# A hybrid encoder layer: raw weights in quarters, gate work moved into branch B, branch A and the output from the last block to the first

## The chip, the cores and the metric

One core of a Trainium2 chip runs the whole layer in one launch. The metric is the device time of one execution in microseconds, median of several runs. The engines are named as in the profile: PE (TensorE matmul), PEld (TensorE weight load), DVE (VectorE), ACT (ScalarE), POOL (GpSimd), SP (SyncE, which here issues every DMA on one queue).

## The reference, cut to what matters

Sequence 2048, model width 1024, float32 throughout, one layer.

```
h    = layer_norm(x)
proj = h @ w_in            # 1024 x 7592, cut into a_*, i_*, b_*, c_* and gate columns
# A: scores of an indexer (8 heads of 32), the 256 best keys of each query,
#    softmax over these; 8 heads of 64 that share one key and one value head
# B: 4 heads, each with two softmaxes p0, p1 over all allowed keys:
#    a = p0 - lam * p1;  o_b = rms_norm(a @ v)          (values 128 wide)
# C: 4 heads of 128, softmax over 256 memory tokens
# allowed keys: s < (t // 64 + 1) * 64, so block b of 128 queries sees (b + 1) * 128 keys
y_r  = (o_r * silu(gate_r)) @ w_proj_r                  for r in A, B, C
merged = sum over r of sigmoid(m_gate_r) * y_r
out  = layer_norm(2 ** 0.25 * h + merged @ w_out)
```

## The kernel before

The 2048 tokens are 16 blocks of 128 queries, or 8 pairs. Every product of the projections is done as three matmuls on a high and a low part (`mm3`, L74 to L77): the weights are read from DRAM in float32 into a raw tile `wr`, and split into `w` by two instructions (`split`, L64 to L72; L67 or L69 makes the high part, L72 the low one). `load_win` (L225) does that for a group of 256 columns: two halves of 512 rows, each one DMA of 512 KB into a raw tile of which there is one buffer, and a split by POOL (in the first part of the kernel ACT makes the high part). The split tile `w` has two buffers, so a group can be loaded while the one before it is in use.

A group of gate columns is a generator, `gate_steps` (L257): 2 x 2 x 8 = 32 steps of three matmuls 128x512, each counted as 0.69 us. There are 20 such groups for each half of the tokens (`JOBS`). Their results go to DRAM (`sg_d`, `tm_d`, `cq_d`).

Order of the program: layer norm and projections of the first half, the indexer's top-k by bisection (`topk_group`), the projections of the second half, top-k of the other blocks, the 20 gate groups of the second half, the first 4 of the first half, then branch B, branch A with what is left of the gates, the memory projections, branches C and B's output (`gated_b`, `gated_c`, called B/C below), and the final stage.

Within branch B (L795 on) the order of TensorE is written out by hand (`manual_schedule`): units of a head and a block, from block 15 to 0, for head 0 to 3. Between their steps `pump` puts gate steps: a unit of block b asks for 3.2 + 0.08 (b + 1) us of them (`FILL`), the first unit's eight logit steps for 0.5 us each. Ten gate groups are kept for this (`GB = (4, 10)`); when they are used up, `pump` does nothing.

Everywhere else a planner sets the order on each engine, SP's queue included: it simulates the program and takes, of the instructions that are ready in the simulation, the one that stands earliest in the program. So the remaining gates, the memory part and B/C, which stand behind branch A in the program, are taken where branch A leaves an engine free. The order so found is fixed: on the chip each engine works it off in turn.

Branch A (`attn_a`, L836) does a block of queries for 8 heads: logits, exponentials, transposes and products with the values. Its pools lie on the right side of the memory, those of B/C and of the first part of the final stage on the left. The final stage has two parts: `stage1(p)` (L1027) needs branch A's output of the pair p (`oa_d`) and the sum of B/C (`mg_d`), and `stage2(b)` (L1082) multiplies by `w_out` and normalizes. The first four `stage1` (`EARLY`) are written so that they need only the left side, whose pools of B/C must have been released; everything after them needs branch A's space as well.

Of the kernel before, what the change touches and what calls it, by code (L numbers as in the profile page):

```python
# [9 lines left out]
F32 = mybir.dt.float32  # L10
# [25 lines left out]
GV = 3  # L36
AHEAD = 1
EARLY = 4
WO = (1, 1)
YT = 8  # L40
YO = 1
APR = 2
GB = (4, 10)
FILL = (3.2, 0.08)
SQ_SCALE = 2.0 ** -80
SQ_LIM = 3.4028234663852886e38 * SQ_SCALE
# [10 lines left out]
def tile_layer(ctx, tc, x, mem, ln_in_g, ln_in_b, w_in, w_mem_kv, diff_lambda, diff_norm_g,  # L57
# [167 lines left out]
    def load_win(cols, eh=G, el=G, rpool=None):  # L225
        w = dw.tile([128, 2, KT, 256], F32R, name="w")
        n = sum(c for _, c in cols)
        for i in range(2):
            if rpool is None:
                raw = dw.tile([128, 4, 256], F32, name="wr", bufs=1)  # L230
            else:
                raw = rpool.tile([128, 4, 256], F32, name="wr")
            o0 = 0
            for c0, cn in cols:
                SP.dma_start(raw[:, :, o0:o0 + cn], w_view(w_in, i * 512, 4, c0, cn))
                o0 += cn
            split(w[:, 0, 4 * i:4 * i + 4, :n], w[:, 1, 4 * i:4 * i + 4, :n], raw[:, :, :n], eh, el)
        return w

    def dense(kind, half, cols, idx, w=None):  # L240
# [25 lines left out]
    def dense_ai01(half):  # L266
        W = []
        for i in range(2):
            if half == 0 and i:
                w = xw.tile([128, 2, 4, W_AI], F32R, name="w1", bufs=1)  # L270
            else:
                w = dw.tile([128, 2, KT, 256], F32R, name="w")
                w = w.rearrange("p a k c -> p (a k c)")[:, :8 * W_AI].rearrange("p (a k c) -> p a k c", a=2, k=4)
            W.append(w)
            for c0, cols in ((0, [(C_AK, 128), (C_IQ, 128)]), (256, [(C_IQ + 128, W_AI - 256)])):
                n = sum(c for _, c in cols)
                raw = dw.tile([128, 4, 256], F32, name="wr", bufs=1)
                o0 = 0
                for a0, an in cols:
                    SP.dma_start(raw[:, :, o0:o0 + an], w_view(w_in, i * 512, 4, a0, an))  # L280
                    o0 += an
                split(w[:, 0, :, c0:c0 + n], w[:, 1, :, c0:c0 + n], raw[:, :, :n], A if half == 0 else G, G)
        for p in range(4 * half, 4 * half + 4):
            ps = [dqs.tile([128, 512], F32, name="dps") for _ in range(2)]
            for a in range(2):
                for i in range(2):
                    h = hT_of(2 * p + i)
                    for k in range(4):
                        kk = 4 * a + k
                        mm3(ps[i][:, :W_AI], h[:, 0, kk], h[:, 1, kk], W[a][:, 0, k], W[a][:, 1, k], kk == 0, kk == KT - 1)  # L290
            with tc.high_priority():
                o = [dw.tile([128, 2, 256], F32, name="do", bufs=3) for _ in range(2)]
                with tc.high_priority():
                    for i in range(2):
                        A.copy(o[0][:, i], ps[i][:, :256])
                        A.copy(o[1][:, i, :W_AI - 256], ps[i][:, 256:W_AI])
                emit("ai0", None, p, None, 256, o[0])
                emit("ai1", None, p, None, W_AI - 256, o[1])
# [82 lines left out]
    def gates(half, jobs, between=()):  # L381
        between = list(between)
        for i, (kind, c0, idx) in enumerate(jobs):
            yield from gate_steps(kind, half, c0, idx)
            if between:
                between.pop(0)()

    def run(steps):
        for _ in steps:
# [12 lines left out]
    def dense_mem(j):  # L402
        w = dw.tile([128, 2, KT, 256], F32R, name="w")
        for i in range(2):
            raw = dw.tile([128, 4, 256], F32, name="wr", bufs=1)
            SP.dma_start(raw, w_view(w_mem_kv, i * 512, 4, 256 * j, 256))
            split(w[:, 0, 4 * i:4 * i + 4], w[:, 1, 4 * i:4 * i + 4], raw, G, G)
        ps = dqs.tile([128, 2, 256], F32, name="dps")
        for i in range(2):
            c = slice(i * 128, (i + 1) * 128)  # L410
            if j < 2:
                for k in range(KT):
                    mm3(ps[:, i], w[:, 0, k, c], w[:, 1, k, c], hm[0][:, 0, k], hm[0][:, 1, k], k == 0, k == KT - 1)
            else:
                for k in range(KT):
                    mm3(ps[:, i], hm[0][:, 0, k, c], hm[0][:, 1, k, c], w[:, 0, k], w[:, 1, k], k == 0, k == KT - 1)
        for i in range(2):
            o = dw.tile([128, 2, 256], F32R, name="do", bufs=3)
            if j < 2:
                split(o[:, 0], o[:, 1], ps[:, i], A, V)  # L420
                SP.dma_start(mk_d[:, 2 * j + i], o.bitcast(F32))
            else:
                h0 = 2 * (j - 2)
                ov = o.rearrange("p a (h d) -> p (a h d)", d=128).rearrange("p (h a d) -> p h a d", h=2, a=2)
                pv = ps[:, i].rearrange("p (h d) -> p h d", d=128)
                split(ov[:, :, 0], ov[:, :, 1], pv, A, V)
                SP.dma_start(mv_d[:, i, h0:h0 + 2].rearrange("p h a d -> p (h a d)"),
                             o.bitcast(F32).rearrange("p a c -> p (a c)"))
# [366 lines left out]
        load_v(0, g)  # L795
    units = [unit_b(hd, b) for hd in range(4) for b in range(NB - 1, -1, -1)]
    with tc.manual_schedule(engines={PE.engine}):
        for _ in units[0].logits():
            pump(0.5)
        units[0].mix()  # L800
        ahead = 1
        for i, u in enumerate(units):
            new = []
            while ahead < len(units) and ahead <= i + 2 and sum(x.slots for x in units[i:ahead + 1]) <= PB:
                new.append(units[ahead])
                ahead += 1
            share = FILL[0] + FILL[1] * (u.b + 1)
            m = 2 * (u.b // 4 + 1)
            n = sum(2 * (x.b // 4 + 1) for x in new)
            lg = (None for x in new for _ in x.logits())  # L810
            j = 0
            nxt = units[i + 1] if i + 1 < len(units) else None
            for t, _ in enumerate(u.values()):
                pump(share / m)
                while (j + 1) * m <= (t + 1) * n:
                    next(lg)
                    j += 1
                if t == m // 2 and nxt is not None and nxt not in new:
                    nxt.mix()
            for _ in lg:  # L820
                pass
            u.store()
            if nxt in new:
                nxt.mix()
# [67 lines left out]
            V.tensor_tensor(oo, oo, rc[:, 4 * h4:4 * h4 + 4, None].to_broadcast([128, 4, 64]), op=ALU.mult)  # L892
        SP.dma_start(oa_d[b], o.rearrange("p h d -> p (h d)"))

    for b in [7, 0, 6, 1, 5, 2, 4, 3, 8, 9, 10, 11, 12, 13, 14, 15]:
        attn_a(b)

    run(fill)
# [143 lines left out]
        return [ap.tile([128, 2, 256], F32, name="facc", bufs=bufs) for _ in range(4)]  # L1042

    wo = []
    for p in range(EARLY):
        acc = accs(fs, 3)
        stage1(p, acc)
        for u in range(4):
            SP.dma_start(mg_d[p][:, 2 * u:2 * u + 2], acc[u])
        if p == WO[0]:  # L1050
            wo += load_w(HW[:, 1], fs, "facc", w_out, 0, 3)
        if p == WO[1]:
            wo += load_w(fw.tile([128, 4, 2, D], F32R, name="wo2"), fs, "facc", w_out, 4, 3)

    aps.release()
# [8 lines left out]

    MT = {}

    def ready(p):
        if p >= NP:
            return
        acc = accs(fp, 4)  # L1070
        if p < EARLY:
            for u in range(4):
                SP.dma_start(acc[u], mg_d[p][:, 2 * u:2 * u + 2])
        else:
            stage1(p, acc)
        MT[p] = fp.tile([128, 2, KT, 256], F32R, name="fmT", bufs=AHEAD + 1)
        for u in range(4):
            H, L = (MT[p][:, a, 2 * u:2 * u + 2] for a in range(2))
            A.activation(H, acc[u], AF.Copy, scale=0.5)
            V.scalar_tensor_tensor(L, acc[u], 0.5, H.bitcast(F32), op0=ALU.mult, op1=ALU.subtract)  # L1080

    def stage2(b):  # L1082
        hh = fp.tile([128, D], F32, name="fh", bufs=3)
        SP.dma_start(hh, h_d[b])
        mT = MT[b // 2][:, :, :, 128 * (b % 2):128 * (b % 2) + 128]
        nz = 4 if b == NB - 1 else 2
        for n in range(nz):
            c = slice(n * (D // nz), (n + 1) * (D // nz))
            z = fq.tile([128, 512], F32, name="fz")[:, :D // nz]
# [1 line left out]
                mm3(z, mT[:, 0, k], mT[:, 1, k], wo[k][:, 0, c], wo[k][:, 1, c], k == 0, k == KT - 1)  # L1091
            V.scalar_tensor_tensor(hh[:, c], hh[:, c], ALPHA, z, op0=ALU.mult, op1=ALU.add)
        mu, rs = norm_stats(fp, hh, nz)
        if b < NB - 1:
            V.tensor_scalar(hh, hh, mu, rs, op0=ALU.subtract, op1=ALU.mult)
            G.tensor_tensor(hh, hh, gln, op=ALU.mult)
            V.tensor_tensor(hh, hh, bln, op=ALU.add)
            SP.dma_start(out[b * 128:(b + 1) * 128, :], hh)
            return
# [6 lines left out]
        ready(p)  # L1106
    for p in range(NP):
        ready(p + AHEAD)
        stage2(2 * p)
        stage2(2 * p + 1)  # L1110
    fq.release()
    fp.release()
    fqr.release()
# [52 lines left out]
```

## Time and profile before

| | us |
|---|---|
| median of 3 runs (lowest, highest) | 3029.1 (3028.67, 3036.97) |
| the profiled execution's own time | 3025.77 |
| its span in the profile | 3024.0 |
| PE busy | 2800.9 (93%) |
| DVE busy | 2165.2 (72%) |
| ACT busy | 1400.3 (46%) |
| POOL busy | 1068.0 (35%) |
| mean granted clock of TensorE | 0.97 of full |

A busy time is the sum over an engine's instructions as the profiler recorded them; matmuls are pipelined and their ends are modelled. The granted clock is told as a share of 2.4 GHz; the two levels seen are full (2.4 GHz) and half (1.2 GHz).

### The profile page before, as it was taken

The numbers are of one execution on the slowest core, as the hardware profiler recorded it, in microseconds if no ns is written. First come the engines' busy times: TensorE is split into PE (matmuls) and PEld (weight loads), VectorE is DVE, ScalarE is ACT, GpSimd is POOL, SyncE is SP. The second block draws the span as 40 slices with busy tenths as digits, with TensorE's granted clock in tenths as the row PEclk, the third lists the DMA queues.
The fourth block names the chain that finished last, engine by engine and source line by source line (L and its number), as shares of the span: only waits on it lengthen the run. The fifth ranks groups of instructions, "written<-read, shape, count | busy, mean of one in ns | idle before, by whom it ended". The sixth has DMA issues, their size and how long they took to land.

```text
span 3024.0 us, 48961 instructions
## 1 busy us (share of the span) xinstructions
PE 2800.9 (93%) x17488; PEld 2503.8 (83%) x17488; DVE 2165.2 (72%) x4885; ACT 1400.3 (46%) x2710; POOL 1068.0 (35%) x1264
## 2 busy tenths in 40 slices
PE   6899889999999998799999997999999999968999
PEld 6898879987788876687878786888898999967887
DVE  7179988999757997577777774447777777745555
ACT  3255654774346870344444443436666565532000
POOL 7443547234423326244353433321222222211222
PEclk9999999999999999899999997999999999989999
DMA  9443434342322354433332323346333333337542
GB/s 327 127 149 133 138 118 135 120 143 93 100 92 85 101 195 132 129 93 114 93 118 86 96 80 105 118 147 188 120 112 104 100 110 91 93 126 238 190 144 86
DMA packets 355027, 383.05 MB, mean 127 GB/s; under 512 B 27872, under 2 KB 283232, under 8 KB 354272
## 3 DMA queue, kind: packets, MB, share of 16 engines
q1 hardware_dynamic: 354784, 379.93, 39.8%
q8 instruction: 138, 2.26, 0.3%
q14 instruction: 105, 0.86, 0.1%
HBM read 240.15 MB, written 139.69 MB: 126 GB/s over the span
## 4 chain that ended last, share of the span: by engine, by line
PE 59%; DVE 16%; DMA 7%; issue 7%; POOL 6%; ACT 4%; SPq 1%; DVEq 0%; POOLq 0%; ACTq 0%
PE dps L76 7%; PE dps L75 7%; PE dps L77 7%; DVE jd L527 5%; PE ops L737 4%; PE aops L881 4%; PE apt L876 3%; PE lg L632 3%; PE lg L633 3%; PE yps L75 3%; PE yps L76 3%; ACT ja L540 3%; PE yps L77 3%; PE pt L745 2%; PE fz L77 2%
## 5 line engine op out<-in xcount | busy, mean ns | idle before, releaser
L75 PE MATMUL dps<-H,w 128*128 128x512 f32 x1280 | 522.0, 408 | 28.5 <-DVE do L315 12.5
L76 PE MATMUL dps<-H,w 128*128 128x512 f32 x1280 | 508.4, 397 | 0.0
L77 PE MATMUL dps<-H,w 128*128 128x512 f32 x1280 | 507.3, 396 | 0.0
L67 POOL TENSOR_SCALAR w<-wr 128x1024 fp32r<-128x1024 f32 x120 | 137.4, 1145 | 657.8 <-PE dps L77 411.3
L75 PE MATMUL dps<-w,H 128*128 128x256 f32 (+1 forms) x1152 | 344.5, 300 | 22.4 <-POOL w L67 7.0
L540 ACT ACTIVATE ja<-sall,thr 128x1280 bf16<-128x1280 f32 (+4 forms) x224 | 302.0, 1348 | 133.6 <-DVE thr L536 124.1
L76 PE MATMUL dps<-w,H 128*128 128x256 f32 (+1 forms) x1152 | 343.8, 299 | 3.9 <-POOL w L72 3.9
L77 PE MATMUL dps<-w,H 128*128 128x256 f32 (+1 forms) x1152 | 341.9, 298 | 3.6 <-DVE H L72 3.5
L72 POOL TENSOR_TENSOR w<-wr,w 128x1024 fp32r<-128x1024 f32 (+1 forms) x128 | 328.6, 2568 | 22.4 <-ACT w L69 14.6
L527 DVE TENSOR_SCALAR_CACHE_REDUCE jd<-sall,thr 128x1408 bf16<-128x1408 f32 (+6 forms) x231 | 330.9, 1433 | 6.7
L75 PEld LDWEIGHTS dps<-H,w 128*128 128x128 f32 x1280 | 245.4, 192 | 76.8 <-DVE do L315 12.9
L77 PEld LDWEIGHTS dps<-H,w 128*128 128x128 f32 x1280 | 244.4, 191 | 51.4
L76 PEld LDWEIGHTS dps<-H,w 128*128 128x128 f32 x1280 | 245.7, 192 | 39.3
L635 DVE CUSTOM_DVE_ANT_0 AP<-lg,bias 128x512 f32<-128x512 f32 (+3 forms) x304 | 182.5, 619 | 95.4 <-PE lg L633 55.5
L500 DVE SCALAR_TENSOR_TENSOR sall<-ir,iw,sall 128x512 f32<-128x512 f32 (+3 forms) x266 | 211.3, 850 | 54.5 <-ACT ir L496 53.2
L75 PEld LDWEIGHTS dps<-w,H 128*128 128x128 f32 x1152 | 225.0, 196 | 26.6 <-POOL w L67 7.7
L72 DVE TENSOR_TENSOR apr<-apt,apr 128x512 fp32r<-128x512 f32 (+1 forms) x288 | 185.5, 656 | 68.4 <-ACT apr L69 66.2
L75 PE MATMUL yps<-yoT,H 128*128 128x256 f32 x768 | 223.5, 292 | 9.8 <-DVE ft L938 6.9
L76 PEld LDWEIGHTS dps<-w,H 128*128 128x128 f32 x1152 | 225.4, 196 | 7.0 <-POOL w L72 6.2
L77 PEld LDWEIGHTS dps<-w,H 128*128 128x128 f32 x1152 | 225.0, 195 | 5.6 <-DVE H L72 4.6
L69 ACT CAST apr<-apt 128x512 fp32r<-128x512 f32 (+1 forms) x288 | 157.5, 564 | 138.8 <-PE apt L876 113.8
L76 PE MATMUL yps<-yoT,H 128*128 128x256 f32 x768 | 220.3, 287 | 1.6 <-POOL yoT L929 1.0
(244 smaller groups left out, 6851.7 us busy)
## 6 DMA issues: line engine op xcount, KB each, us to landing
wr<-in_w_in_dram SPq DMA_DIRECT2D x112, 512.0 KB, 3.7
tm_d<-do SPq DMA_DIRECT2D x96, 256.0 KB, 2.0
bq<-qb_d SPq DMA_DIRECT2D x128, 128.0 KB, 3.0
aq<-qa_d SPq DMA_DIRECT2D x128, 128.0 KB, 3.1
yt<-tm_d SPq DMA_DIRECT2D x64, 256.0 KB, 3.2
sg_d<-do SPq DMA_DIRECT2D x48, 256.0 KB, 2.3
ys<-sg_d SPq DMA_DIRECT2D x48, 256.0 KB, 3.2
facc<-mg_d SPq DMA_DIRECT2D x48, 256.0 KB, 4.6
```

What stands on the lines that cost most here:

```text
L67: G.tensor_scalar(H, src, 1.0, 1.0, op0=ALU.mult, op1=ALU.mult)
L69: A.copy(H, src)
L72: el.tensor_tensor(L, src, H.bitcast(F32), op=ALU.subtract)
L75: PE.matmul(ps, lH, rH, start=start, stop=False)
L76: PE.matmul(ps, lH, rL, start=False, stop=False)
L77: PE.matmul(ps, lL, rH, start=False, stop=stop)
L500: V.scalar_tensor_tensor(s[:, c0:c0 + cn], r[:, :cn], iw[:, h:h + 1], s[:, c0:c0 + cn], op0=ALU.mult, op1=ALU.add)
L527: V.tensor_scalar(jd[:, :L], sc[b], t.bitcast(F32)[:, i:i + 1], None, op0=op, op1=ALU.add, accum_out=dst[:, i:i + 1])
L540: A.activation(ja[:, :L], sc[b], AF.Sign, bias=thr.bitcast(F32)[:, i:i + 1], scale=-1.0, accum_out=cnt[:, i:i + 1])
L635: V.tensor_tensor_reduce(P[:, c0:c0 + cn], ps[:, :cn], bias[:, c0:c0 + cn], scale=-0.125, scalar=-LOW, op0=ALU.add, op1=ALU.min, accum_out ...
L737: PE.matmul(o_ps.rearrange("p a d -> p (a d)"), pr[:, a, i], v, start=(k0 + i == 0 and a == 0), stop=(k0 + i == b and a == 1))
L881: PE.matmul(o_ps.rearrange("p a d -> p (a d)"), VA[:, k0 + i], pr[:, a, i].rearrange("p e q -> p (e q)"), start=(k0 + i == 0 and a == 0), ...
```

## The change

- The raw tile holds two of the eight row tiles of a group instead of four, and has two buffers instead of one; `load_win`, the loads of `dense_ai01` and of `dense_mem` do four quarters (256 KB each for 256 columns) where they did two halves. The very first group, which has its own pool, keeps its halves.
- Two more gate groups are kept for branch B: `GB = (4, 12)`. Four groups are left behind branch A, where there were six. As five functions of the memory part are hung between the groups, the fifth now runs after the last group.
- Branch B begins with `pump(10.0)`, and its first unit's logit steps pump 1.0 us each.
- `attn_a` runs from block 15 down to 0 (before: 7, 0, 6, 1, 5, 2, 4, 3, 8, ..., 15).
- The final stage takes the pairs from 7 down to 0; the block whose end is written out in pieces is the last one done, block 1. B/C still goes from pair 0 to 7.

```diff
+PORD = list(range(NP - 1, -1, -1))
+LAST = 2 * PORD[-1] + 1
-GB = (4, 10)
+GB = (4, 12)
...
-        for i in range(2):
-            if rpool is None:
-                raw = dw.tile([128, 4, 256], F32, name="wr", bufs=1)
-            else:
-                raw = rpool.tile([128, 4, 256], F32, name="wr")
+        m = 2 if rpool is None else 4
+        for i in range(0, KT, m):
+            raw = (rpool or dw).tile([128, m, 256], F32, name="wr", bufs=2)
...
-                SP.dma_start(raw[:, :, o0:o0 + cn], w_view(w_in, i * 512, 4, c0, cn))
+                SP.dma_start(raw[:, :, o0:o0 + cn], w_view(w_in, i * 128, m, c0, cn))
...
-            split(w[:, 0, 4 * i:4 * i + 4, :n], w[:, 1, 4 * i:4 * i + 4, :n], raw[:, :, :n], eh, el)
+            split(w[:, 0, i:i + m, :n], w[:, 1, i:i + m, :n], raw[:, :, :n], eh, el)
...
             if between:
                 between.pop(0)()
+        for f in between:
+            f()
...
     with tc.manual_schedule(engines={PE.engine}):
+        pump(10.0)
         for _ in units[0].logits():
-            pump(0.5)
+            pump(1.0)
...
-    for b in [7, 0, 6, 1, 5, 2, 4, 3, 8, 9, 10, 11, 12, 13, 14, 15]:
+    for b in range(NB - 1, -1, -1):
         attn_a(b)
...
-    for p in range(EARLY):
+    for i in range(EARLY):
+        p = PORD[i]
...
-    def ready(p):
-        if p >= NP:
+    def ready(i):
+        if i >= NP:
             return
+        p = PORD[i]
...
-        if p < EARLY:
+        if i < EARLY:
...
-        nz = 4 if b == NB - 1 else 2
+        nz = 4 if b == LAST else 2
...
-        if b < NB - 1:
+        if b != LAST:
...
         ready(p + AHEAD)
-        stage2(2 * p)
-        stage2(2 * p + 1)
+        stage2(2 * PORD[p])
+        stage2(2 * PORD[p] + 1)
```

## Rows read from the trace of the kernel before

**Rows 1.** Busy time and count of each engine, granted clock, DMA, in chosen stretches

```profile
core 0: us, PE busy (x) PEld busy (x) DVE busy (x) ACT busy (x) POOL busy (x), PEclk, DMA share, GB/s
1220.00:1250.00 30.00, 13.77 (x47) 10.68 (x46) 12.02 (x31) 5.37 (x6) 6.83 (x4) 0.73 0.56 159
1820.00:1860.00 40.00, 23.42 (x125) 19.95 (x123) 24.96 (x88) 14.31 (x40) 24.38 (x53) 0.73 0.27 84
1860.00:1880.00 20.00, 18.01 (x59) 14.00 (x60) 2.92 (x10) 2.60 (x5) 0.28 (x1) 0.78 0.68 187
1880.00:2160.00 280.00, 272.26 (x1742) 241.98 (x1741) 157.44 (x501) 140.74 (x328) 68.49 (x48) 0.99 0.47 145
2160.00:2685.00 525.00, 513.20 (x3951) 483.92 (x3950) 386.82 (x1018) 305.06 (x690) 121.06 (x122) 1.00 0.31 95
2685.00:2795.00 110.00, 72.42 (x465) 66.43 (x464) 48.02 (x70) 23.56 (x40) 13.74 (x11) 0.81 0.73 240
```

**Rows 2.** Gate matmuls in the order of time on PE, around the end of branch B

```profile
1818.18 0.39 PE L77 MATMUL dps<-H,w 128*128 128x512 f32 x1
...
1820.44 0.39 PE L75 MATMUL dps<-H,w 128*128 128x512 f32 x1
...
1825.74 0.39 PE L77 MATMUL dps<-H,w 128*128 128x512 f32 x1
...
1860.18 0.77 PE L75 MATMUL dps<-H,w 128*128 128x512 f32 x1 [0.64 <-DVE hm L72]
```

**Rows 3.** PE's waits from 1100 to 1300 us: total, times, longest

```profile
PE lg L632 <- DMA bq<-qb_d: 9.7, 1, 9.7
...
PE pt L745 <- DVE P L726: 6.6, 1, 6.6
```

**Rows 4.** SP's queue in order of time, at the head of branch B

```profile
1203.89 0.40 SPq L235 DMA_DIRECT2D wr<-in_w_in_dram  x1
...
1230.47 0.54 SPq L235 DMA_DIRECT2D wr<-in_w_in_dram  x1
```

**Rows 5.** POOL in order of time, at the head of branch B

```profile
1234.62 1.05 POOL L67 TENSOR_SCALAR w<-wr 128x1024 fp32r<-128x1024 f32 x1 [21.12 <-DMA wr<-in_w_in_dram]
```

**Rows 6.** The matmuls of branch A with the values (aops), in two stretches

```profile
1880.00:2160.00 280.00, 51.71 (x288) 41.55 (x288) 11.88 (x32) 0.99 0.47 145
2160.00:2685.00 525.00, 153.89 (x800) 116.66 (x800) 11.79 (x32) 1.00 0.31 95
```

**Rows 7.** SP's queue in order of time, where branch A and B/C end

```profile
2684.81 0.33 SPq L893 DMA_DIRECT2D oa_d<-ao  x1
...
2696.16 0.32 SPq L1018 DMA_DIRECT2D mg_d<-yt  x1
2698.34 0.32 SPq L1032 DMA_DIRECT2D fo<-oa_d  x1
```

**Rows 8.** PE's waits from 2685 to 2800 us

```profile
PE gT L925 <- DMA fo<-oa_d: 14.9, 2, 12.1
```

**Rows 9.** PE's waits from 0 to 500 us

```profile
PE dps L75 <- POOL w L67: 7.0, 2, 4.0
PE dps L75 <- ACT w L69: 6.3, 2, 5.0
```

**Rows 10.** Groups of instructions: count, busy us, mean ns, idle before

```profile
L72 POOL TENSOR_TENSOR w<-wr,w 128x1024 fp32r<-128x1024 f32 (+1 forms) x128 | 328.6, 2568 | 22.4 <-ACT w L69 14.6
...
L67 POOL TENSOR_SCALAR w<-wr 128x1024 fp32r<-128x1024 f32 x120 | 137.4, 1145 | 657.8 <-PE dps L77 411.3 <-DMA wr<-in_w_in_dram 213.1 <-DMA wr<-in_w_mem_kv_dram 33.3
...
L929 POOL TENSOR_TENSOR yoT<-ys,yoT 128x512 fp32r<-128x512 f32 x32 | 43.9, 1373 | 239.5 <-ACT yoT L928 237.3 <-PE aops L881 2.2
```

**Rows 11.** DMA issues by line: count, KB each, median us from issue to landing

```profile
wr<-in_w_in_dram SPq DMA_DIRECT2D x112, 512.0 KB, 3.7
...
wr<-in_w_in_dram SPq DMA_DIRECT2D x8, 256.0 KB, 4.2
```

More of the change, by code (lines that the diff above doesn't have):

```diff
@@ L276, in dense_ai01 @@
                 n = sum(c for _, c in cols)
[L277 to L282, printed above, removed]
+                for k in (0, 2):
+                    raw = dw.tile([128, 2, 256], F32, name="wr", bufs=2)
+                    o0 = 0
+                    for a0, an in cols:
+                        SP.dma_start(raw[:, :, o0:o0 + an], w_view(w_in, i * 512 + k * 128, 2, a0, an))
+                        o0 += an
+                    split(w[:, 0, k:k + 2, c0:c0 + n], w[:, 1, k:k + 2, c0:c0 + n], raw[:, :, :n], A if half == 0 else G, G)
         for p in range(4 * half, 4 * half + 4):
@@ L404, in dense_mem @@
         for i in range(2):
-            raw = dw.tile([128, 4, 256], F32, name="wr", bufs=1)
-            SP.dma_start(raw, w_view(w_mem_kv, i * 512, 4, 256 * j, 256))
-            split(w[:, 0, 4 * i:4 * i + 4], w[:, 1, 4 * i:4 * i + 4], raw, G, G)
+            for k in (4 * i, 4 * i + 2):
+                raw = dw.tile([128, 2, 256], F32, name="wr", bufs=2)
+                SP.dma_start(raw, w_view(w_mem_kv, k * 128, 2, 256 * j, 256))
+                split(w[:, 0, k:k + 2], w[:, 1, k:k + 2], raw, G, G)
         ps = dqs.tile([128, 2, 256], F32, name="dps")
@@ L1049, in tile_layer @@
             SP.dma_start(mg_d[p][:, 2 * u:2 * u + 2], acc[u])
-        if p == WO[0]:
+        if i == WO[0]:
             wo += load_w(HW[:, 1], fs, "facc", w_out, 0, 3)
-        if p == WO[1]:
+        if i == WO[1]:
             wo += load_w(fw.tile([128, 4, 2, D], F32R, name="wo2"), fs, "facc", w_out, 4, 3)
```

## The prediction

> **What bounds the kernel now.** I read the time by stretches first, then PE's waits, then the queues at the places that these two point to. PE bounds nearly everything: in the longest stretch, branch A beside B/C, it is busy 513.20 of 525 us at full clock, and 272.26 of 280 in the stretch before it [rows 1]. There the reader is to see that time falls only if work is taken away. So the change must be judged at the few places where PE stands. Three lie where the change acts: the head of branch B (13.77 us busy of 30, clock 0.73), its tail (23.42 of 40, 0.73, and the 20 us behind it still at 0.78), and the passage from A and B/C to the final stage (72.42 of 110, clock 0.81) [rows 1]. Together they hold 16.2 + 16.6 + 2.0 + 37.6 = 72.4 us of idle PE, and some more in matmuls at half clock.
>
> The total of PE's work isn't changed: the same matmuls, the same transposes. What can be won is idle time and half clock at these places; what can be lost is new idle time where work has been taken out.
>
> **The change part by part.**
>
> *How much moves.* Gate matmuls start 0.226 us apart (ten gaps in 2.26 us [rows 2]), so a group of 32 x 3 takes 21.7 us, and two take 43.4. By the program's own count (0.69 us for a step) ten groups supply 220.8 us of fill; branch B asks for 4 (first unit) + 4 x (16 x 3.2 + 0.08 x 136) = 252.3. So today the fill is gone before the end, and the trace shows where: the last gate matmul of B starts at 1825.74, the next one at 1860.18, behind B [rows 2]. After the change twelve groups supply 265.0, and B asks for 10 + 8 + 248.3 = 266.3: the fill lasts to the last unit. Of the 44.2 us that B gets more, 14 go to the head and 30.2 to the tail.
>
> *Tail of B.* From 1820 to 1860 PE was busy 23.42 us at a mean clock of 0.73, which is some 17 us of work at full clock. With 30.2 us of fill that is 47; if PE is then 95% full, a little under its share in A's stretch [rows 1], it takes 50 us instead of 40. So of 30.2 us, 20 cost nothing: **-20 us** in all. At the least favourable the fill steps stand in front of the short chains of the small blocks (matmul, DVE, exponential, transpose, matmul) and delay each of them; then half of it, -10. The most is the whole loss, 16.6 idle and 6.3 of clock, -23.
>
> *Behind the tail.* From 1860 to 1880 the clock is 0.78, because PE stood before; busy 18.01 of 20. If PE keeps working through the tail, 2.0 + 18.01 x 0.22 = 6 us are to be had: I take **-5**, between 0 and -6. The first loads of A (which now are those of block 15, its mask twice as long as block 7's) lie under gate matmuls as before.
>
> *Head of B.* PE waits 9.7 us for the first queries and 6.6 us for the first weights' chain (mix, then transposes) [rows 3]. Ten microseconds of gate steps ahead of the logits fit the first wait. But these steps need their weights: the second half of this group's raw load is issued at 1230.47, behind the keys, values and queries, 26.6 us after the first [rows 4], and POOL waits 21.12 us for it, until 1234.62 [rows 5]. The first four steps (2.7 us) need the first half alone; the fifth stands until the second half or, now, the third quarter has come. PE takes its instructions in order, so what is queued behind such a step is the first logits, then all of B. Two raw buffers let two quarters be asked for early, and the first group's load now stands ahead of the queries' in the program, but behind the keys and values. From +6 (fill stalls as long as the queries did, and the logits come later) to -13 (both waits half gone, clock kept): **-5**. The doubled pump between the logit steps I cost at nothing: it only uses fill earlier.
>
> *Two groups out of A's stretch.* There PE is 97 to 98% busy [rows 1], so 43.4 us less work is 43.4 us less time; this is the other side of the two terms above (B longer by 44.2 - 20 - 5 = 19, A's stretch shorter by 43), and isn't counted again. It holds only while A's stretch has enough other work; see the rivals.
>
> *Order of A, and of the output.* Branch A's last output is stored at 2684.81, the last sum of B/C at 2696.16, and the first load of `stage1` is issued at 2698.34 [rows 7]: both end together, and the passage stands bare. PE waits 12.1 us for that load alone [rows 8], and the stretch from 2685 to 2795 loses 37.6 us plus part of 72.42 x 0.19 = 14 by the clock, say 45 in all. In the new order the small blocks come last. Beside them A uses less of PE: 288 value matmuls in 280 us, against 800 in 525 beside the large ones (1.03 against 1.52 per us) [rows 6], so the fill goes faster there. Fill is now short by 43 us; so B/C should end before A, and the passage, with the first four `stage1` (their outputs of A, pairs 7 to 4, being long stored), can run beside A's last blocks on the other side of the memory. It hides as much of the 45 us as A has left by then: between 0 and -45. Against it: `stage1` of pair 7 reads the sum that B/C has just written, and its load stands in SP's queue until the store has landed, with every other load behind it. The planner draws up the whole order anew, and nothing in the trace says which side ends first: **-20**, a little under half, with a bound of +10 for the wait on pair 7's sum. The order of `stage2` itself costs nothing: the same instructions, and its loads of `h` lie far ahead.
>
> *Quarters.* POOL does 126 more L72 and about 118 more L67. Two L72 of half the size cost 2 x 1373 - 2568 = 178 ns more than one (by the 128x512 form of L929), so 22 us; L67 of half size isn't in the trace: between 0 and the same 178 ns each, 0 to 21 us. That is 22 to 43 us on an engine that is 65% idle, and of L67's 657.8 us of idle time 411.3 are waits for PE to free the tile [rows 10]; so it hides, save in the first 70 us, where a handful of instructions lie on the path: +1. SP issues some 130 more DMAs of about 0.4 us [rows 4], 52 us over the whole span, beside other work. What it buys: a load can run while the quarter before is split, and the first matmul needs a quarter, not a half. PE's waits for split weights are 7.0 and 6.3 us, all before 500 us [rows 9]. Half of that goes: **-6**, with bounds of +4 and -13.
>
> Here the trace and the Trainium skill can be weighed. A raw load of 512 KB lands in 3.7 us and one of 256 KB in 4.2 [rows 11]: halving the size doesn't halve the time. The Trainium skill (DMA: Bandwidth & Descriptors, "Anatomy of one DMA — SWDGE (gpsimd) path") says so in general: about 2.0 us fixed for a DMA, and the bytes at 436 GB/s on top. By it a group's two halves would take an estimated 6.4 us in turn and four quarters 10.4, and if two buffers overlapped none of this, the four exposed loads would each be some 4 us later: by that rule alone the term would be up to +16 instead of -6. I keep -6, since two quarters are in flight at once.
>
> *Sum.* -20 - 5 - 5 - 20 - 6 = -56 us against the profiled execution's own 3025.77: 2970. The median of the runs shown, 3029.1, is 3.3 above that execution; on that scale the forecast is **2973 us**.
>
> **The rivals.**
>
> 1. *The passage stays bare.* A and B/C end together again, as they do now [rows 7]; only B's terms and the weights count: -36, 2993 us. For it: list order shares PE between them all along, and both shrink. Against it: the fill has lost 43 us and A nothing.
> 2. *The passage is wholly covered.* -20 becomes -45: 2948 us. For it: the small blocks leave room, and four `stage1` are ready for it. Against it: the loads of `stage1` come through one queue, and the memory of B/C must be free first.
> 3. *Slower: A's small blocks run bare at the end.* Place: from the last store of B/C to the last of A. If B/C is used up beside the large blocks, nothing but four `stage1` is left beside the small ones, whose chains (logits, minimum, exponential, transposes, splits, values) leave PE idle. The nearest row is B's tail without fill, 23.42 busy of 40, or 41% lost. The eight small blocks took 280 us with company; alone I put them between 150 and 200. At 150 us bare the price is +62 on rival 1: 3055 us. It decides from 110 us on, where 45 us are lost and 2993 becomes 3038. Against it: the planner takes fill only where A is not ready, and the large blocks use more of PE per us.
> 4. *No change.* The same with some 90 us bare (37 lost): 3030 us. That the gates aren't moved as counted would end here too: if the fill stalls in B's head and delays the tail's chains, +6 and -10 stand for -5 and -20.
>
> **How the numbers follow.** Forecast (2973, its own spread 2960 to 2985) 0.38; rival 1 0.22; rival 2 0.13; rival 4 0.12; rival 3 0.15. A change within 0.3% (9 us, from 3020 to 3038) is about what can't be told from none: faster 0.38 + 0.22 + 0.13 = 0.73, same 0.12, slower 0.15. The range takes in rival 2 with the bounds of the small terms below (2935) and rival 4 above (3040), and leaves out rival 3 and a few hundredths at the low end.
>
> **What would show it.** Right: gate matmuls on PE until within 5 us of B's last unit, and no half clock there; B longer by about 19 us; A's stretch shorter by about 43; the last `mg_d` store of B/C before the last `oa_d` store, with `stage1` matmuls between A's; fewer than 25 us idle in the passage. Wrong: a wait of a gate matmul for `w` at B's head as long as the one for queries was (that term is nothing); PE below 80% busy in A's last 100 us (rival 3); A and B/C ending within 12 us of each other and the wait for `fo` still there (rival 1). If PE's waits for `w` before 500 us don't fall below 13 us, the quarters bought nothing.

## The result and the profile after

| | before | after |
|---|---|---|
| median of 4 runs, us (lowest, highest) | 3030.72 (3028.67, 3036.97) | 2954.75 (2948.86, 2959.4) |
| ratio, 95% interval | | 0.9745 [0.9722, 0.9768] |
| span in the profile, us | 3024.0 | 2952.8 |
| PE busy | 2800.9 (93%) | 2785.7 (94%) |
| POOL busy | 1068.0 (35%) | 1140.0 (39%) |
| mean granted clock | 0.97 | 0.98 |

The changed kernel is 76 us faster. The forecast of 2973 was 18 us too long; the time lies inside the range, between the forecast's own spread and the mark of rival 2. The sum was near, but its terms were not: what follows shows one term nine times too small and others that came to nothing.

Read first the stretches that answer to [rows 1], shifted to where the same work now lies (busy us and count of each engine, granted clock, DMA share, GB/s):

```profile
core 0: us, PE busy (x) PEld busy (x) DVE busy (x) ACT busy (x) POOL busy (x), PEclk, DMA share, GB/s
1196.00:1226.00 30.00, 25.38 (x108) 19.89 (x107) 13.24 (x37) 7.16 (x9) 11.28 (x12) 0.95 0.41 121
1774.00:1814.00 40.00, 40.00 (x215) 34.21 (x215) 20.93 (x85) 13.90 (x40) 24.91 (x55) 1.00 0.31 91
1814.00:1834.00 20.00, 15.30 (x62) 11.41 (x60) 0.00 (x0) 1.79 (x3) 8.93 (x13) 0.92 0.81 242
1834.00:2655.00 821.00, 783.86 (x5724) 726.45 (x5724) 561.85 (x1550) 449.28 (x1027) 189.56 (x191) 0.98 0.39 118
2656.00:2745.00 89.00, 71.78 (x427) 64.80 (x428) 45.67 (x70) 20.35 (x34) 12.17 (x10) 0.88 0.84 272
```

B's head (first line) went from 13.77 to 25.38 us busy of 30, its tail (second) from 23.42 to 40.00 of 40 at full clock. The fourth line is the one to look at twice: A's stretch, which has gate work taken out, is not shorter. Its counterpart in the kernel before, in the same view:

```profile
1870.00:2685.00 815.00, 794.59 (x5721) 733.09 (x5722) 546.46 (x1526) 447.64 (x1020) 189.55 (x170) 1.00 0.37 112
```

815 us at full clock have become 821 at 0.98, and PE's idle time in them 37 us instead of 20. The number of matmuls is the same because other work has moved in. Here are the gate matmuls and those of B/C and `stage1` with the output weights (one of the three products of each), before and then after:

```profile
L75 PE MATMUL dps<-H,w 128*128 128x512 f32 x151 | 60.1, 398 | 0.0
L75 PE MATMUL yps<-yoT,H 128*128 128x256 f32 x498 | 144.8, 291 | 1.8 <-DVE yt L938 1.6
```

```profile
L77 PE MATMUL dps<-H,w 128*128 128x512 f32 x96 | 38.0, 396 | 0.9 <-DVE hm L74 0.9
L77 PE MATMUL yps<-yoT,H 128*128 128x256 f32 x544 | 158.2, 291 | 0.6 <-DVE yt L943 0.6
```

That is 165 gate matmuls fewer (37 us at 0.227 us each, not the 43.4 of two groups) and 140 others more (16 us): the stretch holds some 19 us less work at full speed.

PE's waits at B's head, from 1180 to 1300 us (total, times, longest) [as rows 3]; the wait for the queries is no longer among them:

```profile
PE pt L749 <- DVE P L730: 3.7, 1, 3.7
PE dps L79 <- POOL w L74: 0.9, 2, 0.6
...
```

In order of time on PE, around the end of B [as rows 2]; the last B value matmul starts at 1810.23, and gate matmuls follow it without a gap:

```profile
1826.36 0.39 PE L78 MATMUL dps<-H,w 128*128 128x512 f32 x1
1826.59 0.39 PE L79 MATMUL dps<-H,w 128*128 128x512 f32 x1
1831.42 1.19 PE L636 MATMUL lg<-KA,aq 128*128 128x512 f32 x2 [4.45 <-DMA aq<-qa_d]
...
1838.05 1.09 PE L182 MATMUL psT<-idf,do 128*128 128x128 f32 x4 [4.31 <-DMA do<-in_mem_dram]
```

So gate work does last to B's end. Counted group by group, the twelve groups end at 1804.2, and a thirteenth, one of the four left behind branch A, follows at once. The kernel before had an extra group too: 1056 gate matmuls, eleven groups and not ten, stand between B's first logits and its last value matmul, the eleventh from 1787 to 1826. The planner had put it there, and neither the text above nor the prediction counts it.

Behind the thirteenth group PE waits 4.45 us for A's first queries and 4.31 us for the memory tokens; its order has nothing else at these places.

SP's queue where A and B/C end [as rows 7]:

```profile
2619.82 0.33 SPq L1023 DMA_DIRECT2D mg_d<-yt  x1
2621.46 0.33 SPq L1037 DMA_DIRECT2D fo<-oa_d  x1
...
2655.54 0.38 SPq L898 DMA_DIRECT2D oa_d<-ao  x1
```

B/C's last sum is stored 35.7 us before A's last output; before, it was 11.4 us behind it. `stage1` runs beside A's last blocks: its first transpose on PE starts at 2625.1, A's last value matmul at 2647.8. PE's waits in the passage, from 2600 to 2760 us (total, times, longest) [as rows 8]:

```profile
PE gT L930 <- DVE ys L932: 13.0, 4, 9.0
...
PE gT L930 <- DMA fo<-oa_d: 0.6, 1, 0.6
```

The wait for `fo` went from 14.9 to 0.6; the next in line is DVE's product in `stage1`, 13.0 us.

PE's waits for split weights from 0 to 500 us [as rows 9]:

```profile
PE dps L77 <- POOL w L69: 5.7, 2, 3.4
...
PE dps L77 <- ACT w L71: 3.4, 2, 2.4
```

13.3 us have become 9.1. A third row, PE's waits for the low part, is left out in [rows 9]: 3.9 us before, 4.1 after. POOL's split instructions and the loads [as rows 10, 11]:

```profile
L74 POOL TENSOR_TENSOR w<-wr,w 128x512 fp32r<-128x512 f32 (+2 forms) x254 | 361.1, 1431 | 17.2 <-ACT w L71 11.0
...
L69 POOL TENSOR_SCALAR w<-wr 128x512 fp32r<-128x512 f32 x240 | 184.9, 778 | 591.7 <-PE dps L79 449.7 <-DMA wr<-in_w_in_dram 125.8 <-DMA wr<-in_w_mem_kv_dram 15.0
```

```profile
wr<-in_w_in_dram SPq DMA_DIRECT2D x220, 256.0 KB, 3.0
```

POOL works longer, yet waits less for loads (125.8 us, before 213.1).

**Where in the run the time is gained.** Each matmul on PE was given its issue interval at full speed (0.227 us for 512 columns, 0.188 for 424, 0.172 for 384, 0.1165 for 256, 0.109 for a transpose, as the traces show them; the few matmuls of 128 columns were counted like a transpose), and the kernels were compared at equal sums of this work. That takes moved work out of the comparison. The steps, in us against the kernel before, worked out from one profiled execution each and rounded; the last five columns are kernels of the next section:

| stretch, by the time before | after | q_only | b_only | q_tail | after_nohead | ord_only |
|---|---|---|---|---|---|---|
| 0 to 808, projections and indexer | -31 | -34 | +3 | -36 | -34 | 0 |
| 808 to 1254, up to behind B's head | -15 | -5 | -20 | -1 | -1 | +2 |
| 1254 to 1869, B to the end of its tail | -33 | -12 | -22 | -34 | -32 | +1 |
| 1869 to 1923, A's start | +9 | 0 | +4 | 0 | -2 | 0 |
| 1923 to 2676, A beside B/C | +7 | +5 | +19 | +11 | +2 | +2 |
| 2676 to 2828, passage | -9 | 0 | -17 | -3 | -6 | +1 |
| sum to the end (the difference of the spans) | -71 | -47 | -34 | -62 | -74 | +6 |

Where A and the passage meet, a split by other values for the transposes (0.06 to 0.115 us) moves up to 3 us from one row to the next. The profiled execution of before is 3 to 7 us below the medians that the ratios rest on, and the others lie up to 8 us from their own, so the sums differ from the measured gains by 5 to 12 us. The expectations below were written with 12 and 10 us for the changed kernel's last two steps, where this count has 7 and 9.

### The profile page after: what moved, and what is told of

Same layout as the page of the kernel before. It is cut to its first block, busy times and chain, and to the rows that moved or that the text cites. A ratio compares the mean times of both kernels' runs of the same rounds, so it can differ in the third digit from the quotient of the medians.

```text
span 2952.8 us, 49447 instructions
## 1 busy us (share of the span) xinstructions
PE 2785.7 (94%) x17488; PEld 2494.6 (84%) x17488; DVE 2130.6 (72%) x4885; ACT 1398.0 (47%) x2716; POOL 1140.0 (39%) x1510
## 4 chain that ended last, share of the span: by engine, by line
PE 57%; DVE 12%; DMA 6%; issue 5%; POOL 4%; ACT 3%; SPq 1%; DVEq 0%; POOLq 0%; ACTq 0%
PE dps L77 6%; PE dps L78 6%; PE dps L79 6%; PE ops L741 4%; DVE jd L531 4%; PE aops L886 4%; PE apt L881 3%; PE lg L636 3%; PE lg L637 3%; PE yps L78 3%; PE yps L77 3%; PE yps L79 3%; PE pt L749 2%; PE fz L79 2%; PE fz L78 2%
## 5 line engine op out<-in xcount | busy, mean ns | idle before, releaser
L69 POOL TENSOR_SCALAR w<-wr 128x512 fp32r<-128x512 f32 x240 | 184.9, 778 | 591.7 <-PE dps L79 449.7
L74 POOL TENSOR_TENSOR w<-wr,w 128x512 fp32r<-128x512 f32 (+2 forms) x254 | 361.1, 1431 | 17.2 <-ACT w L71 11.0
L77 PE MATMUL yps<-yoT,H 128*128 128x256 f32 x768 | 223.5, 293 | 4.5 <-DVE ft L943 3.9
L886 PE MATMUL aops<-apr,VA 128*128 128x256 f32 x1088 | 208.8, 299 | 16.9 <-ACT apr L71 6.7
```

The lines of the kernel that those rows point to most:

```text
L69: G.tensor_scalar(H, src, 1.0, 1.0, op0=ALU.mult, op1=ALU.mult)
L74: el.tensor_tensor(L, src, H.bitcast(F32), op=ALU.subtract)
L77: PE.matmul(ps, lH, rH, start=start, stop=False)
L886: PE.matmul(o_ps.rearrange("p a d -> p (a d)"), VA[:, k0 + i], pr[:, a, i].rearrange("p e q -> p (e q)"), start=(k0 + i == 0 and a == 0), ...
```

## The experiments

Theory: the parts act as forecast, the tail of B most. Its rival after the result: the quarters carry most of it, because the stretch ahead of B, where only they act, gained 31 us. Line numbers shift by a few between kernels. The median of the kernel before was 3032.43, 3029.36 and 3029.22 us in the three series: one for q_only, no_q, b_only and ord_only, one for q_1buf, h_qsplit, q_b and after_nohead, one for the other four; each ratio goes by its own series.

**Quarters alone** (q_only): before, with

```diff
-        for i in range(2):
-            if rpool is None:
-                raw = dw.tile([128, 4, 256], F32, name="wr", bufs=1)
...
+        m = 2 if rpool is None else 4
+        for i in range(0, KT, m):
+            raw = (rpool or dw).tile([128, m, 256], F32, name="wr", bufs=2)
...
```

> The kernel before with the raw quarters and two buffers alone. Theory (by equal PE work the changed kernel is 31 us ahead before branch B's head, with nothing but the quarters changed there, and gains 6 more inside B): 2990 to 3000 us, and the last indexer matmul some 33 us earlier than 945.2. Rival (the prediction's size for the weights, the 31 us being another order that the planner found because of the later edits): 3020 to 3028, last indexer matmul within 10 us of 945.

**All but the quarters** (no_q): the changed kernel with these lines undone.

> The changed kernel with the raw halves and one buffer of before: everything but the quarters. Theory: the quarters' 37 us come back, 2985 to 2998 us. Rival (the prediction's sizes): 2957 to 2965. If head and tail of branch B need the quarters (their weights come late without them), above 3000.

**Branch B's part alone** (b_only): before, with

```diff
-GB = (4, 10)
+GB = (4, 12)
...
+        pump(10.0)
         for _ in units[0].logits():
-            pump(0.5)
+            pump(1.0)
```

> The kernel before with twelve gate groups for branch B and the pumps at its head alone. Theory (head -17 and tail -16 by equal PE work, these not needing the quarters): 2993 to 3002 us. Rival (the head's gain comes from the quarters, since its weights come late without them): 3005 to 3015, with a wait of gate matmuls for w at B's head.

**The two orders alone** (ord_only): before, with

```diff
-    for b in [7, 0, 6, 1, 5, 2, 4, 3, 8, 9, 10, 11, 12, 13, 14, 15]:
+    for b in range(NB - 1, -1, -1):
...
+PORD = list(range(NP - 1, -1, -1))
```

> The kernel before with branch A and the output from the last block to the first alone. Theory (by equal PE work A's stretch lost 12 us and the passage gave back 10): within 6 us of before, 3025 to 3036. Rival (the prediction's term): 3005 to 3015. Second rival (the order pays only together with two gate groups less behind A, since with six groups B/C ends after A): slower, 3035 to 3050.

| kernel | us | ratio [95%] |
|---|---|---|
| q_only | 2978.95 | 0.9828 [0.9806, 0.9849] |
| no_q | 2988.67 | 0.9864 [0.9845, 0.9883] |
| b_only | 2990.82 | 0.9859 [0.9835, 0.9882] |
| ord_only | 3030.78 | 0.9995 [0.9984, 1.0007] |

Quarters alone are worth 53 us, B's part alone 42, the orders nothing that can be told. q_only came out 11 us below its expected range and b_only 2 below; no_q and ord_only lie inside theirs. The two that count would add to 95; together they gave 80 (q_b, below), so they share some 15.

Where the quarters save can be read in a stretch of equal work, 1243 matmuls of the first projections and the indexer (1240 in q_only's record): first the kernel before, then q_only.

```profile
233.00:417.00 184.00, 162.06 (x1243) 157.52 (x1242) 169.21 (x348) 115.75 (x246) 84.97 (x115) 0.96 0.39 128
```

```profile
225.00:389.00 164.00, 155.36 (x1240) 152.37 (x1239) 153.18 (x344) 114.77 (x245) 89.98 (x139) 1.00 0.44 143
```

164 us instead of 184: 13.3 less idle, and 6.7 less busy because the clock no longer falls (0.96 to 1.00). PE's waits in these stretches, before and then q_only:

```profile
PE psT L216 <- POOL do L139: 5.3, 6, 1.5
PE dps L75 <- DVE pre L545: 5.1, 1, 5.1
PE dps L75 <- POOL w L67: 4.0, 1, 4.0
```

```profile
PE dps L75 <- DVE de L72: 2.9, 2, 2.2
PE dps L75 <- POOL w L67: 2.0, 1, 2.0
PE psT L216 <- POOL do L139: 1.7, 4, 0.8
```

Only 2 of the 13 us are waits named after `w`. 3.6 are a wait for another job of POOL (`do`, L139, the rotation of queries and keys), and 5.1 one for DVE (another, for `de`, grew by 2.2). Over the whole stretch up to 808 us of before, with 4903 matmuls in both kernels, PE's idle time fell by 24 us, of which 16 stand in waits for DVE and 7 in waits for POOL. So the gain stands in rows that do not bear the split's name. That the splits held up what was queued behind them would explain this; but the planner's order changed as well, and these rows do not part the two.

**What in the quarters: the loads or the splits?** q_1buf keeps the quarters and takes the second buffer away (its edit is shown against q_only); h_qsplit keeps the loads of before (512 KB, one buffer) and splits each half in two pieces; h_qsplit_rev has `(2, 0)` where h_qsplit has `(0, 2)` and so does the later piece first, so that the first matmul again waits for the whole half. All three do the same in `dense_ai01` and `dense_mem`.

```diff
-            raw = (rpool or dw).tile([128, m, 256], F32, name="wr", bufs=2)
+            raw = (rpool or dw).tile([128, m, 256], F32, name="wr", bufs=1 if rpool is None else 2)
```

> The kernel before with the raw weights in quarters, but one raw buffer (half the memory): each quarter is loaded after the one before it has been split. Theory 1 (the gain of 53 us of the quarters comes from loads that run during splits): most of it is gone, 3015 to 3040 us. Theory 2 (it comes from POOL's shorter instructions, between which rope and other work gets in sooner): most of it stays, 2980 to 2995.

```diff
-            split(w[:, 0, 4 * i:4 * i + 4, :n], w[:, 1, 4 * i:4 * i + 4, :n], raw[:, :, :n], eh, el)
+            for k in (0, 2) if rpool is None else ():
+                split(w[:, 0, 4 * i + k:4 * i + k + 2, :n], w[:, 1, 4 * i + k:4 * i + k + 2, :n], raw[:, k:k + 2, :n], eh, el)
...
```

> The kernel before with its loads of 512 KB and one raw buffer, but each half split in two pieces of a quarter. Theory 1 (loads during splits): no gain, 3020 to 3040 us. Theory 2 (shorter POOL instructions, and the first matmul needs a quarter only): most of the 53 us, 2980 to 3000.

> As h_qsplit (loads of 512 KB, one raw buffer, each half split in two pieces), but the piece with the later rows of a half is split first, so that the first matmul of a group waits for the whole half as it does before the change. Theory a (the shorter splits pay since the first matmul starts after a quarter): most of h_qsplit's 39 us is lost, 3015 to 3030 us. Theory b (they pay since POOL's other work, rope above all, gets in between, and the planner can place it better): it stays, 2985 to 3000.

| kernel | us | ratio [95%] |
|---|---|---|
| q_1buf | 3020.89 | 0.9965 [0.9952, 0.9979] |
| h_qsplit | 2990.46 | 0.9871 [0.9857, 0.9886] |
| h_qsplit_rev | 3007.24 | 0.9925 [0.9911, 0.9938] |

q_1buf falls into the range of its theory 1, h_qsplit into that of its theory 2, and h_qsplit_rev between its two. Shorter splits with untouched loads give 39 of the 53 us. Of these 22 stay when the first matmul must wait for the whole half; the other 17 go with its earlier start, in kernels that the planner has each ordered anew. PE's waits for `w` by 500 us were 13.8 us in h_qsplit (the two rows that read 13.3 before), while its time fell by 39: those rows do not measure what the splits cost. Nor does the row of the rotations, in the same stretch, before and then h_qsplit:

```profile
PE psT L216 <- POOL do L139: 19.7, 14, 3.1
```

```profile
PE psT L216 <- POOL do L139: 19.5, 11, 3.7
```

So the size of the gain is measured and its way to PE is not traced. Quarters without the second buffer lose nearly all (8 us are left): PE's two rows for `w` by 500 us grow to 21.8, and POOL's row shows the loads behind them (busy, mean ns, idle time by releaser); q_only, q_1buf, h_qsplit in turn:

```profile
L67 POOL TENSOR_SCALAR w<-wr 128x512 fp32r<-128x512 f32 x240 | 187.2, 788 | 575.8 <-PE dps L77 434.8 <-DMA wr<-in_w_in_dram 129.0 <-DMA wr<-in_w_mem_kv_dram 11.3
```

```profile
L67 POOL TENSOR_SCALAR w<-wr 128x512 fp32r<-128x512 f32 x240 | 161.9, 674 | 748.3 <-DMA wr<-in_w_in_dram 482.7 <-PE dps L77 219.5 <-DMA wr<-in_w_mem_kv_dram 39.8
```

```profile
L67 POOL TENSOR_SCALAR w<-wr 128x512 fp32r<-128x512 f32 x240 | 179.3, 765 | 621.3 <-PE dps L77 384.8 <-DMA wr<-in_w_in_dram 206.9 <-DMA wr<-in_w_mem_kv_dram 29.4
```

With one buffer POOL waits 482.7 us for loads, with two 129.0; with halves and one buffer 206.9 (213.1 before). So in these kernels small loads cost more than halves unless two are in flight, and small loads with the second buffer give the last 14 us. Two buffers of halves, which take twice the memory, were not tried; so how much of the 14 is the buffer and how much the smaller loads is open.

**Smaller still** (q_b_e8): eighths of 128 KB, four buffers, on q_b.

> q_b (quarters, twelve groups, pumps, old orders) with the raw weights in eighths of 128 KB and four buffers in the same memory. Theory b (shorter POOL instructions pay): some of the next halving too, 2930 to 2945 us. Rival (the fixed cost of POOL's instructions and of twice as many loads on SP's queue takes it back): 2950 to 2975.

2954.15 us, 0.9747 [0.9733, 0.9762]: no better than quarters (q_b, 2949.29), as its rival said.

**Pumps and orders beside the quarters.** q_b is the changed kernel with the old orders, after_nohead the changed kernel without `pump(10.0)` and with 0.5 us a logit step, q_tail has neither the pumps nor the orders.

> The changed kernel with the old order of branch A and of the output: quarters and branch B's gates alone. Theory (the two orders are worth nothing, as they were on the kernel before: -2 us): 2950 to 2960 us, as the changed kernel. Rival (the order pays only with fewer gates behind A): 2970 to 2980. Second rival (small blocks last cost more than the passage gives back): 2935 to 2947.

> The changed kernel without the pumps at branch B's head (no 10 us ahead, 0.5 us per logit step as before); twelve groups stay, so the fill is not quite used up in B. Theory (with the quarters the head's weights and loads come in time, and by equal PE work the pumps are worth some 5 us there): 2957 to 2965 us. Rival (the head's 17 us by equal work come from the pumps): 2970 or more.

> The kernel before with the quarters and twelve gate groups for branch B alone: no pumps at B's head, old orders. Theory (neither pumps nor orders are worth anything): 2945 to 2955 us, as q_b and the changed kernel. Rival (one of them is needed where the other is missing): 2960 or more.

| quarters and 12 groups, us (ratio, 95%) | old orders | new orders |
|---|---|---|
| pumps of before | 2955.83 (0.976 [0.9743, 0.9776]) | 2950.03 (0.9743 [0.9721, 0.9765]) |
| new pumps | 2949.29 (0.9737 [0.9722, 0.9751]) | 2954.75 (0.9745 [0.9722, 0.9768]) |

The intervals overlap, and the small differences have no common sign: with quarters and `GB = (4, 12)` alone one has the whole change, as far as some 5 us can be told. after_nohead came out 7 us below its expected range, q_b and q_tail within 1 us of theirs.

Why the pumps' gain of some 13 us at the head does not reach the end can be read at A's start. First the changed kernel, then after_nohead; each window begins some 3 us behind B's last value matmul:

```profile
1814.00:1845.00 31.00, 21.92 (x92) 16.28 (x90) 5.48 (x16) 5.99 (x11) 12.69 (x17) 0.83 0.76 234
```

```profile
1807.00:1838.00 31.00, 31.00 (x139) 25.69 (x138) 4.16 (x13) 5.85 (x10) 9.70 (x15) 1.00 0.71 216
```

Without the pumps B leaves part of its fill over (349 gate matmuls come after A's first logits, 288 with them), and gates run on through A's first loads. With the pumps PE stands there 9 us, and the clock falls with it: 11 of the 13 us are lost again in the step of A's start (+9 against -2; q_b and q_tail, the same pair with the old orders, have +10 and 0). The gap has moved from B's head to A's.

The order's part in the passage is settled by SP's queue. b_only, old orders:

```profile
2655.20 5.90 SPq L1021 DMA_DIRECT2D mg_d<-yt  x2
2661.14 0.43 SPq L1035 DMA_DIRECT2D fo<-oa_d  x1
2700.72 0.41 SPq L896 DMA_DIRECT2D oa_d<-ao  x1
```

Here B/C also ends first, 40 us ahead (its last store is the second of the two in the first line, at 2660.77), without the new order. ord_only has the new order and the old fill, and both end together:

```profile
2701.62 0.33 SPq L1020 DMA_DIRECT2D mg_d<-yt  x1
2703.70 0.33 SPq L895 DMA_DIRECT2D oa_d<-ao  x1
2704.20 0.32 SPq L1034 DMA_DIRECT2D fo<-oa_d  x1
```

And q_tail, with the same twelve groups, ends the other way round, with the wait for the first load (PE's waits, 2600 to 2760) as before:

```profile
2626.02 0.33 SPq L895 DMA_DIRECT2D oa_d<-ao  x1
2637.45 0.32 SPq L1020 DMA_DIRECT2D mg_d<-yt  x1
2641.68 0.32 SPq L1034 DMA_DIRECT2D fo<-oa_d  x1
```

```profile
PE gT L927 <- DMA fo<-oa_d: 12.3, 1, 12.3
```

q_tail's passage is bare (-3 in the table of steps, where the changed kernel has -9) and its A ends earlier; its time is within 1.1 us of the changed kernel's. So in these kernels a covered passage won nothing: where it is covered, A's start and stretch take longer.

**More of the passage to hide** (q_b_early6): q_b with `EARLY = 6`, so that six `stage1` may run beside A.

> q_b with six stage1 before branch A's space is released instead of four. Theory (B/C ends 30 us before A in q_b, and two more stage1 fill what is left of A): 2940 to 2950 us. Rival (A is over by then, and their round trip through DRAM only lengthens the passage): 2950 to 2960.

2950.91 us, 0.974 [0.9724, 0.9755]: nothing more. No kernel of this study beats the changed one by more than the intervals allow.

## Why the prediction was right in sum and wrong in its terms

- **Tail of B, -20: right.** b_only gains 22 us from 1254 to 1869, q_tail 34 to q_only's 12, again 22, near the bound of -23. The mechanism is as told: gate matmuls to the end, 40.00 of 40 busy, clock 1.00. The count of the fill was not: the kernel before already had an eleventh group in the tail, so B got 120 gate matmuls more up to its last value matmul (1176 for 1056), 27 us and not 44.2.
- **Behind the tail, -5: wrong.** The clock from 1814 to 1834 did rise (0.92, before 0.78), but PE then waits 4.45 us for A's queries and 4.31 for the memory tokens, and the step from 1869 to 1923 is +9, not -5. Without the pumps it is -2.
- **Head of B, -5: met at first, then lost again.** The head gained 15, with 25.38 us busy instead of 13.77; without the pumps (q_tail) 1. Yet the time with and without pumps is the same (the table of four), because the fill spent at the head is missing at A's start. PE's fill stalls there were 0.9 us, far from the wait that I had feared: the wait for queries is gone and the one for `P` is 3.7 (6.6 before).
- **"43.4 us less work is 43.4 us less time": not met.** The prediction named the condition, enough other work, and then left it at nothing. By equal work A's stretch comes out 7 us worse in the changed kernel, 19 in b_only and 11 in q_tail, but 2 in after_nohead, and 5 in q_only, which took no gates out. PE's share fell from 97.5 to 95.5% and the clock to 0.98 in the changed kernel. That the missing fill does it is likely and not shown: the planner drew up each order anew. It is not rival 3: in the 100 us before A's last store PE is busy 91.57.
- **Order of A and of the output, -20: wrong.** The passage was covered (78.2 us from A's last store to the first matmul of `stage2` became 38.1), but ord_only is worth -1.7 us [-4.8, +2.1 by its interval], and the cover comes with the old order too. What the passage gave, -9, A's start and stretch took, +9 and +7.
- **Quarters, -6: the term that was mis-sized.** They are worth 53 alone. I took the price from PE's waits named after `w` before 500 us, 13.3 us, and halved it. Those rows do not hold the price: h_qsplit gains 39 us and leaves them where they were. A split of 128x1024 holds POOL for 1.15 us (high part) and then 2.57 (low part), and in q_only the time is won in PE's waits for DVE and for POOL's rotations, and in the clock (0.96 to 1.00 in the stretch shown). That long splits held up what was queued behind them fits this; beside it the planner's other order remains. The cost bound of +4 held: POOL's 72 us more (I had 22 to 43) are hidden.
- **The sum.** -6 became -53; -5 behind the tail, -5 at the head and -20 in the order became about nothing: -56 forecast, -76 measured. The two errors had opposite signs, and so the sum was closer than its terms. That is luck.
- **The rivals.** Rival 4 says that +6 and -10 for -5 and -20 would end at no change; with the other terms as forecast that sum is -35, some 2994 us, so it priced no second way to 3030.
- **My tests.** Gate matmuls to B's end at full clock, `mg_d` before `oa_d`, and fewer than 25 us idle in the passage (17.2) came true. "Waits for `w` below 13 us" came true with 9.1 by the two rows, and failed with 13.2 by all three (17.2 before); either way it was a poor test: h_qsplit fails it with 13.8 and gains 39 us. "A's stretch shorter by 43" failed, and B was 15 shorter (640.2 to 625.4 us from its first logit to A's), not 19 longer: q_only, with the old fill, has 628.8.

What stays open: of the 22 us that are left in h_qsplit_rev, how much is shorter blocking in POOL's queue and how much the planner's other order. Shorter instructions change both at once, and no run holds one of them fixed. Open too is what A's stretch loses to the missing fill and what to its new order.

## What to carry to other kernels

Do not price a long instruction by the waits that bear its output's name alone: halving POOL's splits paid 39 us with POOL 35% busy, while those waits stayed. Pair smaller loads with a second buffer; without it q_1buf kept 8 of the 53 us. And where two streams share an engine, look for where a closed gap opens again: the fill spent at B's head was missing at A's start. Compare kernels at equal work done, for that shows it.

## What the runs showed of the hardware

- Half the size was not half the time on POOL: TENSOR_TENSOR 128x512 took 1431 ns against 2568 for 128x1024, TENSOR_SCALAR 778 against 1145 [rows 10]. In the changed kernel two small ones cost 294 and 411 ns more than one large one; the prediction had 178, from another line, and 0 to 178.
- A raw load of 256 KB landed in 3.0 us (220 loads), against 3.7 for 512 KB and not the 4.2 of the eight loads in [rows 11]. The Trainium skill (DMA: Bandwidth & Descriptors, "Anatomy of one DMA — SWDGE (gpsimd) path") would make the two 2.6 and 3.2, an estimate from its 2.0 us and 436 GB/s: 0.4 to 0.5 less than the trace, with about the same difference. It states this fit for DMAs issued by GpSimd, and the prediction took it as general; these are issued by SyncE. A fixed part paid by each load in turn is in line with q_1buf, some 42 us over q_only.
